# A decoder layer in fp32: softmax scalings made for two query blocks at once, and the next group's left weights moved behind an operand in a load queue

## The chip, the cores and the metric

The kernel runs on one core of a Trainium2 chip. The metric is the time of one execution on the device in microseconds (us); less is better. A core has TensorE (PE, matrix products; PEld is its loading of weights), VectorE (DVE), ScalarE (ACT), GpSimd (POOL) and SyncE (SP), which here only issues loads and stores. Each engine works through its own instructions in order and waits for others by semaphores.

## What is computed

The reference is one inference step of a decoder layer with 1024 prompt tokens and 8 sample tokens of width 1024, all in fp32. Three parts add to the residual: a mixer whose input projection feeds four heads of differential attention and four of retention, a cross-attention into 256 memory tokens, and a squared-ReLU MLP with 4096 hidden rows. The change touches the first and the last:

```python
def diff_attention(q, k, v, q_pos, k_pos, rel_bias, lam):
    q1, q2 = q[..., :DK_A], q[..., DK_A:]
    k1, k2 = k[..., :DK_A], k[..., DK_A:]
    ...
    def probs(qi, ki):
        s = jnp.einsum('bqhd,bkhd->bhqk', qi, ki).astype(f32) * scale + bias
        return jax.nn.softmax(jnp.where(mask, s, neg), axis=-1)

    attn = probs(q1, k1) - lam * probs(q2, k2)
    return jnp.einsum('bhqk,bkhd->bqhd', attn, v.astype(f32))

def sq_relu_mlp(h, w_up, w_down):
    return jnp.square(jax.nn.relu(h @ w_up)) @ w_down
```

The heads' outputs are then divided by their root mean square (`head_rms`).

## The kernel before

Every fp32 product is made of three matmuls on halves: an operand is split into a rounded high half (a cast on ACT) and the rest (a subtraction on DVE), here UH/UL, wh/wl, KA/KB or ah/al.

**The softmax stage** lies at about 250 to 416 us. The prompt attention works per head `h`, query block `q` of 128 rows and map `m` (0 and 1) in `scores` (L1006): PE makes the scores `sp` in PSUM, with one instruction DVE adds the bias and mask `M` and finds the row's extreme (L1019), and ACT takes the exponential with the row sums `sm` (L1025). After map 1, DVE makes a factor per row, lambda times one sum over the other, by a reciprocal (L1032) and a small scalar_tensor_tensor (L1033), and adds the scaled second map to the first (L1034), so that one unnormalized map `e0` is left. `turn` (L1037) transposes `e0` of a pair of blocks on PE (`trA`), splits it into `ah` and `al`, and `weigh` multiplies by the values. When a head is through, ACT squares its output (`sq`, L1077 in `norm_sums`), PE sums the squares by columns (`ct`, in `norm_factors`), and the factors of the norm are spread out again through a transpose (`hrT`).

A loop over 40 steps walks through heads and pairs and interleaves these pieces with other work (projections of the following heads, `qkp`, retention). The order of PE's matmuls is pinned to the program's; the other engines are ordered by a scheduler, under the waits that data and buffers make. Tiles come from rings: `mn` (maxima and factors) has four, the second maps `e1` have two, which the squares `sq`, and the later `rbh` and `diag` share.

**The down projection** is the last stage, from 1133 us on. Its products are made over quadrants in the manner of Strassen: seven products q = 1 to 7, on sums of quadrants of the weights (left) and of the hidden rows (right, in the scratch HQ and HT in DRAM). A loop runs over four groups `g` of 1024 hidden rows. `load_left` loads a group's eight left tiles `raw_d` (512 KB each, L2492); `right_lower` loads a right operand in two halves `raw_h` (516 KB each, L2375), from a ring of three tiles, casts (L2381) and subtracts (L2382); `left_lower` splits a left tile (L2388, L2389); `lower` makes twelve matmuls (L2412) into a bank `dn`, and DVE adds the bank to a quadrant `c` of the output (L2546). The quadrants begin with the residual, which SP loads (`c<-X3`, L2361). All these loads stand in SP's one queue. Where the program says `issue_after(x)`, the scheduler puts an instruction behind x; `seen["SP"]` is the last load that `right_lower` or `load_left` issued. In group 0 the operands come in the order 1, 2, 6, 7, 4, 5, 3.

## Time and profile before

| | |
|---|---|
| median of 3 runs | 1473.42 us (1473.18 to 1474.27) |
| the profiled execution | 1475.19 us |
| its span | 1473.4 us |
| mean granted clock of TensorE | 0.996 |
| instructions | 28129 |
| moved by DMA | 238.98 MB, mean 162 GB/s |

The span reaches from the first to the last instruction of the profiled execution; what lies around it makes up the rest of its time. A row of the timeline gives start, duration, engine, line of the kernel, operation, output<-inputs with their sizes, and in brackets the idle time ahead of it with what ended that. PE and PEld rows overlap, as matmuls are pipelined. The granted clock is the share of TensorE's full rate. SPq rows are the issue of loads, not their running.

### The profile page before, as it was taken

The numbers are of one execution on the slowest core, as the hardware profiler recorded it, in microseconds if no ns is written. First come the engines' busy times: TensorE is split into PE (matmuls) and PEld (weight loads), VectorE is DVE, ScalarE is ACT, GpSimd is POOL, SyncE is SP. The second block draws the span as 40 slices with busy tenths as digits, with TensorE's granted clock in tenths as the row PEclk, the third lists the DMA queues.
The fourth block names the chain that finished last, engine by engine and source line by source line (L and its number), as shares of the span: only waits on it lengthen the run. The fifth ranks groups of instructions, "written<-read, shape, count | busy, mean of one in ns | idle before, by whom it ended". The sixth has DMA issues, their size and how long they took to land.

```text
span 1473.4 us, 28129 instructions
## 1 busy us (share of the span) xinstructions
PE 1455.7 (99%) x11013; PEld 1401.0 (95%) x11013; DVE 1107.9 (75%) x2263; ACT 679.7 (46%) x1327; POOL 314.4 (21%) x345
## 2 busy tenths in 40 slices
PE   9999999999999999999999999999999999999998
PEld 7899779999889999999999999999999999999998
DVE  7666536888867756567868988888888878787876
ACT  7434435666552441267436533343435443343454
POOL 0035433122304511224122000000002211110380
PEclk9999999999999999999999999999999999999998
DMA  8155738215957265654762444333446764536273
GB/s 295 62 188 171 205 70 192 72 34 159 283 169 269 100 209 170 177 178 122 236 234 77 151 159 158 138 136 133 149 159 216 262 213 144 173 105 200 71 130 116
DMA packets 129833, 238.98 MB, mean 162 GB/s; under 512 B 13606, under 2 KB 80987, under 8 KB 129572
## 3 DMA queue, kind: packets, MB, share of 16 engines
q1 hardware_dynamic: 91354, 170.66, 36.0%
q0 software_dynamic: 27472, 46.93, 11.8%
q10 hardware_dynamic: 10874, 19.60, 3.5%
q8 instruction: 86, 1.41, 0.4%
q14 instruction: 47, 0.39, 0.1%
HBM read 171.13 MB, written 58.92 MB: 156 GB/s over the span
## 4 chain that ended last, share of the span: by engine, by line
PE 88%; DVE 5%; DMA 2%; ACT 2%; issue 1%; POOL 0%; ACTq 0%; SPq 0%; DVEq 0%
PE dn L2412 20%; PE Z L2244 9%; PE qkp L75 6%; PE Y L2244 6%; PE X L2244 6%; PE mq L75 6%; PE pr_m L75 6%; PE pr_o L75 5%; PE grp L75 3%; PE sp L75 2%; PE mv L75 2%; PE mk L75 1%; PE av L75 1%; PE mpv L75 1%; PE vap_z L524 1%; PE vrp_z L524 1%
## 5 line engine op out<-in xcount | busy, mean ns | idle before, releaser
L2412 PE MATMUL dn<-UH,wd 128*128 128x258 f32 (+1 forms) x1800 | 326.6, 283 | 3.0 <-DVE c L2546 3.0
L2412 PEld LDWEIGHTS dn<-UH,wd 128*128 128x128 f32 x1800 | 279.6, 190 | 3.6 <-ACT wd L2388 2.6
L2412 PE MATMUL dn<-UL,wd 128*128 128x258 f32 x900 | 254.6, 283 | 0.0
L2412 PEld LDWEIGHTS dn<-UL,wd 128*128 128x128 f32 x900 | 170.5, 189 | 0.1
L2546 DVE TENSOR_TENSOR c<-c,dn 128x258 f32<-128x258 f32 (+1 forms) x217 | 89.1, 417 | 38.5 <-PE dn L2412 35.8
L2270 ACT ACTIVATE hq<-r 128x258 f32<-128x258 f32 x128 | 53.7, 421 | 117.4 <-DVE r L2269 117.3
L2244 PE MATMUL Z<-T_h,wu 128*128 128x258 f32 x512 | 98.1, 283 | 0.0
L2244 PE MATMUL X<-UH,wu 128*128 128x258 f32 x512 | 97.5, 282 | 0.0
L2388 ACT CAST wd<-raw_d 128x512 fp32r<-128x512 f32 x96 | 58.7, 619 | 82.0 <-PE dn L2412 77.3
L2052 ACT CAST wu<-raw_up 128x512 fp32r<-128x512 f32 x96 | 59.0, 616 | 61.0 <-PE Z L2244 52.6
L2381 ACT CAST UH<-raw_h 128x1032 fp32r<-128x1032 f32 x56 | 58.7, 1055 | 55.2 <-PE dn L2412 27.9
L2244 PEld LDWEIGHTS X<-UH,wu 128*128 128x128 f32 x512 | 81.3, 188 | 0.0
L2244 PEld LDWEIGHTS Z<-T_h,wu 128*128 128x128 f32 x512 | 81.3, 189 | 0.0
L2382 DVE TENSOR_TENSOR UL<-raw_h,UH 128x1032 fp32r<-128x1032 f32 x56 | 72.9, 1301 | 9.9 <-ACT UH L2381 9.9
L2389 DVE TENSOR_TENSOR wd<-raw_d,wd 128x512 fp32r<-128x512 f32 x96 | 72.3, 759 | 10.2 <-ACT wd L2388 10.2
L2281 POOL DMA_DIRECT2D HT<-ht x32 | 17.2, 536 | 292.1 <-DVE ht L2280 291.6
L2244 PE MATMUL Z<-T_l,wu 128*128 128x258 f32 x256 | 72.3, 282 | 0.0
L2244 PE MATMUL X<-UL,wu 128*128 128x258 f32 x256 | 72.3, 282 | 0.0
L129 ACT CAST wh_u<-raw_u 128x1024 fp32r<-128x1024 f32 x43 | 44.7, 1047 | 57.6 <-PE mq L75 39.9
L2053 DVE TENSOR_TENSOR wu<-raw_up,wu 128x512 fp32r<-128x512 f32 x96 | 64.8, 689 | 3.6 <-ACT wu L2052 3.6
L2402 POOL TENSOR_TENSOR raw_d<-raw_d,raw_d 128x512 f32<-128x512 f32 x16 | 22.1, 1384 | 197.0 <-DVE raw_d L2398 145.3
L130 DVE TENSOR_TENSOR wl_u<-raw_u,wh_u 128x1024 fp32r<-128x1024 f32 x39 | 48.6, 1257 | 20.2 <-ACT wh_u L129 20.0
(616 smaller groups left out, 4707.4 us busy)
## 6 DMA issues: line engine op xcount, KB each, us to landing
raw_u<-in_wall SPq DMA_DIRECT2D x49, 512.0 KB
HT<-ht POOLq DMA_DIRECT2D x32, 516.0 KB, 3.0
raw_h<-HT SPq DMA_DIRECT2D x32, 516.0 KB
raw_up<-in_wall SPq DMA_DIRECT2D x32, 512.0 KB
raw_d<-in_wall SPq DMA_DIRECT2D x32, 512.0 KB
HQ<-hq ACTq DMA_DIRECT2D x32, 387.0 KB
raw_h<-HQ SPq DMA_DIRECT2D x24, 516.0 KB
cmk<-in_cmk SPq DMA_DIRECT2D x16, 512.0 KB
```

Of the source, the lines that this page charges most:

```text
L75: pinned(nc.tensor.matmul(out, l, r, start=start, stop=stop))
L130: (lo_engine or nc.vector).tensor_sub(wl[:, :n], raw[:, :n], wh[:, :n].bitcast(F32))
L2052: nc.scalar.copy(w[:, :512], src)
L2053: nc.vector.tensor_sub(w[:, 512:], src, w[:, :512].bitcast(F32))
L2244: pinned(nc.tensor.matmul(ps, l, r[:, k, :], start=first and k == 0 and x == 0, stop=k == 3 and x == 2, skip_group_check=True))
L2270: nc.scalar.activation(h[:, PLACE[quad], :], r, AF.Square)
L2381: nc.scalar.copy(h, rv)
L2382: nc.vector.tensor_sub(l, rv, h.bitcast(F32))
L2388: nc.scalar.copy(w[:, :512], src)
L2389: nc.vector.tensor_sub(w[:, 512:], src, w[:, :512].bitcast(F32))
L2412: pinned(nc.tensor.matmul(ps[:, part], l, r[:, k, cq], start=first and k == 0 and x == 0, stop=k == 3 and x == 2, skip_group_check=True))
L2546: nc.vector.tensor_add(y, y, ps)
```

## The change

The reciprocal and the small product of L1032 and L1033 are made once for a pair of blocks, on two columns, after map 1 of the odd block; the two scalings of the pair (in the changed kernel L1037) follow there. In the down projection the left tiles of group 1 are placed behind group 0's last operand load.

```diff
             if m:
-
-                e0 = es[h, q][0]
-                nc.vector.reciprocal(mn[:, 2:3], sm[:, 1, q : q + 1])
-                nc.vector.scalar_tensor_tensor(mn[:, 3:4], mn[:, 2:3], nlam, sm[:, 0, q : q + 1], ALU.mult, ALU.mult)
-                nc.vector.scalar_tensor_tensor(e0[:, :n], e[:, :n], mn[:, 3:4], e0[:, :n], ALU.mult, ALU.add)
+                es[h, q] += (e,)
+            if m and q % 2:
+                nc.vector.reciprocal(mn[:, 2:4], sm[:, 1, q - 1 : q + 1])
+                nc.vector.scalar_tensor_tensor(mn[:, 2:4], mn[:, 2:4], nlam, sm[:, 0, q - 1 : q + 1], ALU.mult, ALU.mult)
+                for x in range(2):
+                    e0, _, e1 = es[h, q - 1 + x]
+                    w = P * (q + x)
+                    nc.vector.scalar_tensor_tensor(
+                        e0[:, :w], e1[:, :w], mn[:, 2 + x : 3 + x], e0[:, :w], ALU.mult, ALU.add)
                 seen["E"] = nc.cur_bb.bb.instructions[-1]
...
-            load_left((0, 1) if g == 0 else range(4))
+            with tc.issue_after(seen["SP"]) if g == 1 else nullcontext():
+                load_left((0, 1) if g == 0 else range(4))
```

The order of PE's instructions is the same in both. SP's queue around group 0's last operand (raw_h0_3_0 and raw_h0_3_2), with the next group's left tiles raw_d1, before:

```order
L2375 DMA raw_h0_5_0_14176<-HT_75 128x4x258
L2375 DMA raw_h0_5_2_14180<-HT_75 128x4x258
L2492 DMA raw_d1_0_0_14436<-in_wall 128x1024
L2492 DMA raw_d1_1_0_14438<-in_wall 128x1024
L2375 DMA raw_h0_3_0_14184<-HQ_74 128x4x258
L2492 DMA raw_d1_2_0_14440<-in_wall 128x1024
L2375 DMA raw_h0_3_2_14188<-HQ_74 128x4x258
L2361 DMA c12_13489<-X3_73 128x516 x4
L2492 DMA raw_d1_0_1_14437<-in_wall 128x1024
L2492 DMA raw_d1_3_0_14442<-in_wall 128x1024
L2375 DMA raw_h1_1_0_14452<-HQ_74 128x4x258
```

And in the changed kernel:

```order
L2379 DMA raw_h0_5_2_14148<-HT_75 128x4x258
L2379 DMA raw_h0_3_0_14152<-HQ_74 128x4x258
L2379 DMA raw_h0_3_2_14156<-HQ_74 128x4x258
L2365 DMA c12_13457<-X3_73 128x516 x4
L2496 DMA raw_d1_0_0_14404<-in_wall 128x1024
L2496 DMA raw_d1_0_1_14405<-in_wall 128x1024
L2496 DMA raw_d1_1_0_14406<-in_wall 128x1024
L2496 DMA raw_d1_1_1_14407<-in_wall 128x1024
L2496 DMA raw_d1_2_0_14408<-in_wall 128x1024
L2496 DMA raw_d1_3_0_14410<-in_wall 128x1024
L2379 DMA raw_h1_1_0_14420<-HQ_74 128x4x258
L2496 DMA raw_d1_2_1_14409<-in_wall 128x1024
```

Three left tiles stood in these rows ahead of raw_h0_3_2, and a fourth, raw_d1_1_1, farther up; now all eight stand behind it. Six stand ahead of the next group's first operand raw_h1_1_0, as before, but in one run, and a seventh has moved ahead of that operand's second half.

ACT at the end of head 0, where its square sq_0 is made while head 1's last blocks are under way (e_1_7_1 is map 1 of head 1's block 7), before:

```order
L1025 ACTIVATE e_1_7_0_3422,sm_1_2936<-e_1_7_0_3422,mn_1_7_3423 128x1024
L1077 ACTIVATE sq_0_3464<-oraw_0_2753 128x1024
L1052 CAST ah_1_2_1_3487<-trA_1_2_1_3482 128x512
L967 CAST KA1_2_3473<-kraw_2_3127 64x688
L1025 ACTIVATE e_1_7_1_3448,sm_1_2936<-e_1_7_1_3448,mn_1_7_3423 128x1024
L1052 CAST ah_1_2_2_3536<-trA_1_2_2_3532 128x384
```

And in the changed kernel:

```order
L1025 ACTIVATE e_1_7_0_3405,sm_1_2928<-e_1_7_0_3405,mn_1_7_3406 128x1024
L967 CAST KA1_2_3457<-kraw_2_3116 64x688
L1056 CAST ah_1_2_1_3471<-trA_1_2_1_3466 128x512
L1025 ACTIVATE e_1_7_1_3431,sm_1_2928<-e_1_7_1_3431,mn_1_7_3406 128x1024
L1081 ACTIVATE sq_0_3448<-oraw_0_2746 128x1024
L1056 CAST ah_1_2_2_3520<-trA_1_2_2_3516 128x384
```

The square has moved behind the exponential of block 7's second map.

DVE at the same place, where head 1's block 6 is scaled (e_1_6_0<-e_1_6_1), before:

```order
L1033 SCALAR_TENSOR_TENSOR mn_1_6_3370<-mn_1_6_3370,nlam_88,sm_1_2936 128x1
L1019 ISA e_1_7_0_3422,mn_1_7_3423<-sp_1_7_0_1_3428,M_1_2934,mn_1_7_3423 128x512
L1019 ISA mn_1_7_3423 128x1
L1034 SCALAR_TENSOR_TENSOR e_1_6_0_3369<-e_1_6_1_3394,mn_1_6_3370,e_1_6_0_3369 128x896
L1019 ISA e_1_7_1_3448,mn_1_7_3423<-sp_1_7_1_0_3449,M_1_2934 128x512
```

And in the changed kernel, where the small instructions are on two columns:

```order
L1032 RECIPROCAL mn_1_7_3406<-sm_1_2928 128x2
L1091 TENSOR_TENSOR c8_1_4067<-c8_1_4067 128x8
L1033 SCALAR_TENSOR_TENSOR mn_1_7_3406<-mn_1_7_3406,nlam_88,sm_1_2928 128x2
L1037 SCALAR_TENSOR_TENSOR e_1_6_0_3355<-e_1_6_1_3380,mn_1_7_3406,e_1_6_0_3355 128x896
L1037 SCALAR_TENSOR_TENSOR e_1_7_0_3405<-e_1_7_1_3431,mn_1_7_3406,e_1_7_0_3405 128x1024
```

The scaling of block 6 has moved behind all four reductions of block 7.

## The prediction

> **What bounds the kernel now.** I read the busy table of the page first.

> ```profile
> PE 1455.7 (99%) x11013; PEld 1401.0 (95%) x11013; DVE 1107.9 (75%) x2263; ACT 679.7 (46%) x1327; POOL 314.4 (21%) x345
> ```

> TensorE (PE) is busy for 1455.7 of 1473.4 us. The change takes no matmul away and leaves their order as it was, so work that it saves on another engine counts only where PE stands waiting for it. The second view is therefore the list of PE's waits (line waited for, total us, times, longest).

> ```profile
> PE dn L2412 <- DVE c L2546: 3.0, 2, 2.4
> PE trA L78 <- DVE e L1034: 2.1, 2, 1.4
> PE sp L75 <- DVE mn L1019: 1.8, 2, 1.0
> PE pr_half L75 <- DVE x_half L1356: 0.6, 1, 0.6
> ```

> The first belongs to the down projection, the others to the softmax stage and the step behind it. Third, the timeline of PE gives each of these gaps its place; the bracket is the idle time ahead of the row and who ended it.

> ```profile
> 262.42 0.41 PE L75 MATMUL sp<-KA,Q 128*128 128x320 f32 x1 [0.85 <-DVE mn L1019]
> 350.06 0.55 PE L78 MATMUL trA<-ident,e 128*128 128x128 f32 x3 [0.73 <-DVE e L1034]
> 390.33 0.41 PE L75 MATMUL sp<-KA,Q 128*128 128x320 f32 x1 [0.98 <-DVE mn L1019]
> 395.97 0.55 PE L78 MATMUL trA<-ident,e 128*128 128x128 f32 x3 [1.40 <-DVE e L1034]
> 414.71 0.42 PE L75 MATMUL pr_half<-UH,wh_u 128*128 128x344 f32 x1 [0.61 <-DVE x_half L1356]
> 1188.26 0.36 PE L2412 MATMUL dn<-UH,wd 128*128 128x258 f32 x1 [2.38 <-DVE c L2546]
> ```

> All that the change can win on PE is in these few places. The largest gap costs more than its own length, as PE's rows behind it and two rows of the windows view show (us, busy time of PE, PEld, DVE, ACT, POOL, granted clock, DMA share, GB/s).

> ```profile
> 1189.17 0.41 PE L2412 MATMUL dn<-UL,wd 128*128 128x258 f32 x1
> 1192.39 0.37 PE L2412 MATMUL dn<-UL,wd 128*128 128x258 f32 x1
> 1192.59 0.40 PE L2412 MATMUL dn<-UH,wd 128*128 128x258 f32 x2
> 1192.95 0.40 PE L2412 MATMUL dn<-UH,wd 128*128 128x258 f32 x2
> 1189.20:1192.40 3.20, 3.20 (x18) 3.20 (x17) 2.06 (x5) 0.00 (x0) 0.00 (x0) 0.50 1.04 376
> 396.60:399.60 3.00, 3.00 (x33) 2.54 (x32) 3.00 (x12) 1.51 (x3) 0.01 (x1) 1.00 1.06 407
> ```

> In the fifth row the granted clock is 0.50. From 1189.17 to 1192.39 the pattern of one UL and two UH matmuls runs five times, so 15 matmuls take 3.22 us, 0.215 each; from 1192.59 to 1192.95 three take 0.36, 0.120 each. The 15 would have taken 1.80 at that pace: 1.42 lost, and 0.08 more with the one that still starts 0.20 ahead of its successor. So the gap of 2.38 brought 1.5 more, 3.9 in all. The last row shows the clock at 1.00 right behind the gap of 1.40 at 395.97: not every gap brings it.

> [...]

> **Part two of the change, the queue of the down projection.** What ends the gap at 1188.26 is the addition into `c`, L2546, and I followed it back through the timelines of ACT, DVE and SP's queue, then the landings in the chain of waits.

> ```profile
> 1185.46 1.05 ACT L2381 CAST UH<-raw_h 128x1032 fp32r<-128x1032 f32 x1 [1.11 <-DMA raw_h<-HQ]
> 1186.55 1.23 DVE L2382 TENSOR_TENSOR UL<-raw_h,UH 128x1032 fp32r<-128x1032 f32 x1 [0.18 <-ACT UH L2381]
> 1187.70 0.42 DVE L2546 TENSOR_TENSOR c<-c,dn 128x258 f32<-128x258 f32 x1
> 1174.51 0.38 SPq L2375 DMA_DIRECT2D raw_h<-HQ  x1
> 1174.93 0.51 SPq L2492 DMA_DIRECT2D raw_d<-in_wall  x1
> 1177.60 0.38 SPq L2375 DMA_DIRECT2D raw_h<-HQ  x1
> 1170.01 5.21 DMA raw_h<-HT
> 1177.60 7.84 DMA raw_h<-HQ
> 1180.10:1185.90 5.80, 5.78 (x49) 5.58 (x47) 2.04 (x3) 2.02 (x3) 0.00 (x0) 1.00 0.78 279
> ```

> The last operand's second half, raw_h0_3_2, is issued at 1177.60 and lands 7.84 later. Its cast and the subtraction UL follow, and in DVE's order the addition of dn_7_2_0 stands behind that subtraction, though it needs nothing of it. PE wants the bank's result at 1185.88 (1188.26 less 2.38) and gets it only then. By SP's order three left weights of the next group, 0.5 MB each, stand close ahead of this load. The change puts all eight behind raw_h0_3_2: the first half still goes at 1174.51, and the second can follow as soon as its slot is free, some 0.5 us earlier at 1177.1 since the queue does nothing in between. The load before them, with little beside it, took 5.21. With that duration, and not 7.84, it lands at 1182.3; at the 279 GB/s of the windows row, the 1.5 MB that no longer run ahead are 5.4 us less, which gives 1180.0. The chain behind it has measured 1188.12 less 1185.44, 2.7 us: the addition ends at 1182.7 to 1185.0, and PE asks at 1185.9. The wait goes, with 0.9 to 3 us to spare. I take the whole **-3.9**; the bounds are -3.9 and, if the second half keeps its landing, 0.

> What is late next? The eight weights now start behind four pieces of c12, and the next group's operands raw_h1_1_0 and raw_h1_1_2 stand behind six and seven of them on SP. In PE's order the first matmul that needs raw_h1_1_2 comes some 11 steps of 12 matmuls (1.45 us each at 0.120) behind 1185.9, at about 1201.9, and cast and subtraction want it landed by 1199.1. From 1174.5 on 6.8 MB must come through (four operand halves of 0.53, c12 with 1.06, seven weights of 0.52): 280 GB/s. I charge nothing, and say below what it costs if that rate fails.

> **Part one, the scaling once per pair.** These are the two removed kinds by the group view of the softmax stage, and one that stays.

> ```profile
> L1033 DVE SCALAR_TENSOR_TENSOR mn<-mn,nlam,sm 128x1 f32<-128x1 f32 x32 | 6.9, 216 | 0.2
> L1032 DVE RECIPROCAL mn<-sm 128x1 f32<-128x1 f32 x32 | 5.1, 160 | 2.1 <-ACT e L1025 2.0
> L1034 DVE SCALAR_TENSOR_TENSOR e<-e,mn,e 128x896 f32<-128x896 f32 x4 | 4.6, 1146 | 0.1
> ```

> Half of the 64 small ones go: 16 x (0.160 + 0.216) = 6.0 us of DVE, with those on 128x2 priced like those on 128x1. PE waits for DVE in this stage for only a few us, so most of the 6.0 lies beside other work. Gap by gap, by DVE's order in the changed program: the one at 262.42 loses the scaling that stood ahead of its reduction (-0.6 of 0.85); those at 350.06 and 395.97 lose a pair of small ones (-0.2 each); the one at 390.33 gets a scaling placed ahead of it (+0.3); at 414.71 the work left over is less (-0.6). That is **-1.3**. Bounds: all five gaps gone, -4.6, and +1 if the later scaling delays a transpose.

> The cost is in a wait that the trace of before does not have. The square `sq` of a head shares the two slots of `e1` with the second maps. In both programs its slot comes free with the scaling of block 6 of the next head. That scaling now waits for block 7's exponential and for the pair's factor. PE's column sums `ct`, in a fixed place, need `sq`. Heads 1 and 2:

> ```profile
> 320.17 0.60 PE L78 MATMUL trA<-ident,e 128*128 128x128 f32 x4
> 320.10 1.05 ACT L1077 ACTIVATE sq<-oraw 128x1024 f32<-128x1024 f32 x1
> 321.05 0.57 ACT L1052 CAST ah<-trA 128x512 fp32r<-128x512 f32 x1
> 322.43 1.15 ACT L1025 ACTIVATE e<-e,mn 128x1024 f32<-128x1024 f32 x1
> 323.49 0.19 ACT L1025 ACTIVATION_READ_ACCUMULATOR e<-e,mn 128x1 f32 x1
> 322.74 1.84 PE L75 MATMUL ct<-ones,sq 128*128 128x1 f32 x16
> 364.26 1.06 ACT L1077 ACTIVATE sq<-oraw 128x1024 f32<-128x1024 f32 x1
> 366.36 1.15 ACT L1025 ACTIVATE e<-e,mn 128x1024 f32<-128x1024 f32 x1
> 366.77 1.84 PE L75 MATMUL ct<-ones,sq 128*128 128x1 f32 x16
> ```

> Before, `sq` began ahead of the exponential of block 7 and `ct` found it ready. After, for the first pair of rows: the transposes end at 320.77, the cast 0.57 gives 321.4 (ACT's order now has it ahead of the exponential), exponential 1.15 + 0.19, reciprocal 0.16, factor 0.22, scaling 1.15, square 1.05: 325.3 against 322.74, so PE waits 2.5. For the next head the exponential can start about 1.6 earlier than its 366.36, since DVE has three instructions fewer ahead of it (0.16 + 0.22 + 1.15): 364.8, plus 1.15 + 0.19 + 0.16 + 0.22 + 1.15 + 1.06 = 3.93, is 368.7 against 366.77: 2.0. Together **+4.5**. If neither exponential starts earlier than it did, they come to 322.43 + 3.92 - 322.74 = 3.6 and 366.36 + 3.93 - 366.77 = 3.5, that is 7.1; if the instructions overlap by 0.1 each, as the two starts 322.43 and 323.49 of a 1.15 do, 3.3. I take 4.5, the value that follows the new order. Work behind `ct` on PE is in order and cannot step in.

> A gap of 2.38 brought the half clock, one of 1.40 did not. Of the new gaps one is longer and one lies between. I count it once: **+1.5**; bounds 0 and 3.0. [...]

> **The sum.** -3.9 - 1.3 + 4.5 + 1.5 = +0.8. On the profiled execution, 1475.19 with a span of 1473.4, that makes 1476.0 and a span of 1474.2. It lies 1.77 above the median of the runs, 1473.42; the same +0.8 there gives **1474.2**.

> **Rivals.**
> 1. *No half clock behind the new gaps.* The 1.40 gap with its clock of 1.00 speaks for it, the 2.38 gap against: -3.9 - 1.3 + 4.5 = -0.7, 1472.7. [...]
> 2. *Half clock behind both.* -3.9 - 1.3 + 4.5 + 3.0 = +2.3, 1475.7; with the longer waits of the upper bound, +4.9, 1478.3.
> 3. *Slower: the wait comes back one group later.* If the transfers hold less than 280 GB/s, raw_h1_1_2 lands late; at 260 the 6.8 MB end at 1200.7, and as its issue also waits for slots, some 2.1 behind 1199.1. Then PE stands 2.1 and runs at half clock for 1.5, and 3.6 of the 3.9 is given back: +4.4, 1477.8. The 279 above speaks for it, the 376 against. The same sum results if the first wait stays.
> 4. *Faster: DVE's relief reaches every gap.* The softmax gaps go whole and neither `ct` draws the half clock: -3.9 - 4.6 + 4.5 = -4.0, 1469.4. That both `sp` gaps are ended by the reduction behind the scaling speaks for it; that the scalings now come two at a time speaks against.
> 5. *The change does nothing on DVE's side* because the pairing is hidden whole and `ct` finds another slot: -3.9, 1469.5. The slot's release is fixed by the ring of two, which speaks against.

> **How the numbers follow.** What a measurement of this kernel can tell from no change is about 0.2%, 2.9 us. Chances: forecast 0.32, rival 1 0.18, rival 2 0.17 (0.10 of it within 0.2%), rival 3 0.18 (slower), rival 4 0.10 and rival 5 0.05 (both faster). No case within 0.2% is left out but that of the longer `ct` waits, 0.03 of the forecast's 0.32, which is slower. So faster 0.15, same 0.32 - 0.03 + 0.18 + 0.10 = 0.57, slower 0.07 + 0.18 + 0.03 = 0.28. The range holds the forecast and rivals 1, 2 and 3; it leaves out rivals 4 and 5 (0.15) and the upper end of rival 2 (about 0.04): 1470.0 to 1478.0.

> **What would show it.** Right: no gap above 0.5 us at the step of 1188; two gaps ahead of `ct`, 2 to 3 us each, ended by ACT's `sq`; a granted clock of 0.50 behind at least one. Wrong: `ct` without a wait, or with more than 3.6; gaps at the start of group 1 ended by `UL`; gaps of the softmax stage that stay as they are, or go whole.

## The result and the profile after

| | median, us | runs |
|---|---|---|
| before | 1473.30 | 1472.53 to 1474.27, 4 runs |
| changed | 1491.65 | 1490.89 to 1496.19, 4 runs |

The ratio is 1.0131, 95% interval 1.011 to 1.0152: 18.4 us slower, where 0.8 us was forecast and 1478.0 was the upper end of the range. The profiled execution of the changed kernel took 1496.19 us with a span of 1494.4, the longest of the four. Medians and ratios below leave out one execution of 2869.56 us in run 9, which the record doesn't explain.

The page of the changed kernel, busy time of each engine:

```profile
PE 1465.8 (98%) x11013; PEld 1408.9 (94%) x11013; DVE 1104.7 (74%) x2231; ACT 680.2 (46%) x1327; POOL 310.5 (21%) x345
```

PE executes the same 11013 matmuls in the same order and is busy 10.1 us longer than its 1455.7 before. So matmuls ran slower. The other half of the loss stands in the list of PE's waits:

```profile
PE trA L78 <- DVE e L1037: 5.9, 5, 3.4
PE ct L75 <- ACT sq L1081: 5.0, 2, 2.8
PE av L75 <- DVE al L1057: 2.1, 1, 2.1
PE dn L2416 <- DVE c L2551: 1.9, 4, 0.6
PE sp L75 <- DVE mn L1019: 1.3, 2, 0.7
```

Before, `trA` waited 2.1, `ct` not at all, `av` 0.3 and `sp` 1.8. So the softmax stage and the step behind it wait 10.1 us more (3.8 + 5.0 + 1.8 - 0.5). In the down projection the wait of 2.4 is gone, and four of up to 0.6 stand there, of which the last, 0.6 at the end of the stage, was there before. The timeline of PE gives the places:

```profile
326.41 2.15 PE L75 MATMUL ct<-ones,sq 128*128 128x1 f32 x16 [2.82 <-ACT sq L1081]
354.90 0.30 PE L78 MATMUL trA<-ident,e 128*128 128x128 f32 x1 [0.79 <-DVE e L1037]
356.51 0.55 PE L78 MATMUL trA<-ident,e 128*128 128x128 f32 x3 [1.30 <-DVE e L1037]
376.00 3.58 PE L75 MATMUL ct<-ones,sq 128*128 128x1 f32 x16 [2.22 <-ACT sq L1081]
409.76 0.31 PE L78 MATMUL trA<-ident,e 128*128 128x128 f32 x1 [3.38 <-DVE e L1037]
430.42 0.43 PE L75 MATMUL pr_half<-UH,wh_u 128*128 128x344 f32 x1 [0.61 <-DVE x_half L1360]
446.03 0.38 PE L75 MATMUL av<-al,VH 128*128 128x256 f32 x1 [2.13 <-DVE al L1057]
786.15 0.75 PE L75 MATMUL pr_m<-UH,wh_u 128*128 128x258 f32 x4 [0.26 <-ACT UH L2175]
1209.56 0.36 PE L2416 MATMUL dn<-UH,wd 128*128 128x258 f32 x1 [0.34 <-DVE c L2551]
```

The `pr_half` row stood at 414.71 before: 15.7 us are lost by then. The row at 1209.56 is the matmul that stood at 1188.26, 21.3 later. The two waits at `ct` are those that were predicted, 2.8 and 2.2 for 2.5 and 2.0. The second `ct` also takes 3.58 us instead of 1.84. The windows view (us, busy time of PE, PEld, DVE, ACT, POOL, granted clock, DMA share, GB/s), put where PE's rows lie twice as far apart:

```profile
328.00:331.40 3.40, 3.40 (x15) 3.34 (x15) 0.94 (x5) 0.50 (x2) 1.66 (x1) 0.50 0.03 5
375.80:379.20 3.40, 3.20 (x15) 3.20 (x16) 1.36 (x2) 1.08 (x2) 0.62 (x2) 0.50 0.52 108
379.20:382.60 3.40, 3.40 (x13) 3.40 (x14) 2.34 (x4) 0.00 (x0) 1.61 (x2) 0.50 0.17 36
409.92:413.32 3.40, 3.13 (x12) 2.99 (x12) 2.87 (x8) 1.63 (x5) 0.00 (x0) 0.50 1.04 396
447.47:450.87 3.40, 3.40 (x17) 3.27 (x16) 0.56 (x1) 0.48 (x1) 0.00 (x0) 0.50 0.11 36
788.80:792.20 3.40, 3.40 (x18) 3.40 (x17) 1.24 (x1) 0.53 (x1) 0.00 (x0) 0.50 0.00 0
```

Six windows of half clock, 3.4 us each, against one before, besides the 0.50 at the end of both spans (from 1488.5 here and from 1465.6 before). Each costs up to half its length by its clock of 0.50, 1.7, so five more make by this estimate some 8.5 of the 10.1; the rest I did not assign. The waits of the softmax stage and the step behind it and the longer busy time together give 20.2 of the 21.0 by which the two spans differ. The rest is mainly what the memory stage waits more (`mtr` from 0.2 to 1.1 and two new waits of 0.3 and 0.4) less the 0.6 that the down projection waits less.

### The profile page after: what moved, and what is told of

The parts are those of the page before. It is cut to its first block, busy times and chain, and to the rows that moved or that the text cites. A ratio compares the mean times of both kernels' runs of the same rounds, so it can differ in the third digit from the quotient of the medians.

```text
span 1494.4 us, 28120 instructions
## 1 busy us (share of the span) xinstructions
PE 1465.8 (98%) x11013; PEld 1408.9 (94%) x11013; DVE 1104.7 (74%) x2231; ACT 680.2 (46%) x1327; POOL 310.5 (21%) x345
## 4 chain that ended last, share of the span: by engine, by line
PE 81%; DVE 8%; DMA 5%; ACT 3%; issue 2%; ACTq 0%; POOL 0%; SPq 0%; DVEq 0%
PE dn L2416 17%; PE Z L2248 9%; PE qkp L75 6%; PE pr_m L75 6%; PE X L2248 6%; PE Y L2248 6%; PE mq L75 5%; PE pr_o L75 5%; PE grp L75 3%; PE sp L75 1%; PE av L75 1%; PE mpv L75 1%; PE vap_z L524 1%; PE vrp_z L524 1%; DMA raw_h<-HQ 1%
## 5 line engine op out<-in xcount | busy, mean ns | idle before, releaser
L75 PE MATMUL qkp<-UH,wh_u 128*128 128x344 f32 x192 | 63.9, 333 | 0.1
```

What stands on the lines that cost most here:

```text
L75: pinned(nc.tensor.matmul(out, l, r, start=start, stop=stop))
```

## The experiments

All medians stand beside runs of the kernel before on the same chip, which gave 1473.2 to 1473.3 in each set. Theory A puts the loss into the new waits of the softmax stage with the half clock behind them; B and the others stand in the texts.

**1. The queue alone.** The kernel before, with part two of the change alone.

> The kernel before with part two alone (the left weights of group 1 behind raw_h0_3_2). Theory A, the loss is part one's and part two gains: the gap of 2.38 us and its half clock of 1.5 go, the four small gaps that the changed kernel shows in the down projection (0.53, 0.34, 0.59, 0.32 us) come, so 1473.3 - 3.9 + 1.8 = 1471.2 us, 1470 to 1472. Theory B, part two carries part of the loss, since the eight weights collide with the next group's operands: 1473.3 us or more.

Measured: 1473.58 us against 1473.29, ratio 1.0004 (0.9995 to 1.0013). The time lies in theory B's range, but the interval holds no change at all: the loss that B means isn't there, nor are the 2 us of gain that A counted on. Its profiled execution has no wait at the old place, 0.6 at the end of the stage and 1.0 near its start (`dn` waiting for ACT's `c`).

**2. The pairs alone.** The changed kernel with the load queue of before (part two taken back).

> The changed kernel with the queue of before (part one alone). Theory A: the whole loss and part two's gain on top, 1491.7 + 2.1 = 1493.8 us, 1492 to 1496, with the gap of 2.4 us in the down projection back. Theory B: clearly under 1490 us.

Measured: 1491.83 us against 1473.29, ratio 1.0136 (1.0119 to 1.0153). Part one is the whole loss; the time is just under the 1492 at which theory A's range begins. The gap of 2.4 in the down projection, which should have come back with the old queue, did not: `dn` waits 0.6 in all, at the end of the stage.

**5. The kernel before, profiled again**, since the first two runs left the gap in doubt.

> The kernel before, unchanged, profiled once more. Theory F, the gap of 2.38 us at 1188 was an event of that one execution and not of the kernel, which is why part two alone gave 1473.58 against 1473.29: no gap over 0.6 us at the same place (between the first matmuls of q = 4 in group 0), profiled time 1471 to 1474 us. Theory G, the gap belongs to the kernel and part two trades it for something else: a gap of 2 us or more there again.

Measured: 1471.85 us, in one execution. Theory F for this execution. Its waits, its second issue of `raw_h` and the casts behind, from three views:

```profile
PE dn L2412 <- DVE c L2546: 0.6, 1, 0.6
```

```profile
1178.72 0.38 SPq L2375 DMA_DIRECT2D raw_h<-HQ  x1
```

```profile
1183.51 1.06 ACT L2381 CAST UH<-raw_h 128x1032 fp32r<-128x1032 f32 x1 [1.11 <-DMA raw_h<-HQ]
```

The 0.6 stands at the end of the stage. The same load, with the same three left weights ahead of it, took 4.8 us from issue to cast instead of 7.86, and PE ran through. A gap of 2.38 belonged to one execution. But theory F goes too far when it calls the gap no matter of the kernel, as PE's rows at the same matmul in runs 9 and 10 show, which have the old queue too:

```profile
1196.87 0.36 PE L2415 MATMUL dn<-UH,wd 128*128 128x258 f32 x1 [1.15 <-DVE c L2549]
1190.82 0.36 PE L2415 MATMUL dn<-UH,wd 128*128 128x258 f32 x1 [0.43 <-DVE c L2549]
```

At this matmul the six executions with the old queue wait 2.38, 0, 0, 1.15, 0.43 and 0, which is 0.7 on average, and of the seven with the new queue one waits 0.34 and the others at most 0.1. So the new queue does nearly clear this place, but `dn` waits elsewhere instead: near the start of the stage, for ACT's `c`, six of the seven wait 0.5 to 1.0, against one of the six with 0.4. Over all profiled executions `dn` waits 3.0, 0.6, 0.6, 1.8, 1.2 and 2.2 us with the old queue (before, its repetition, and runs 2, 9, 10 and 11) and 2.4, 1.6, 2.2, 1.7, 2.9, 1.5 and 1.8 with the new one (changed, runs 1, 3, 4, 6, 7, 8). In sum the new queue takes nothing off.

**3. The last pair single.** The changed kernel, where blocks 6 and 7 are scaled one by one, so that the slot of `e1` comes free as it did before:

```diff
-            if m and q % 2:
+            n_ = 2 if q < 6 else 1
+            if m and (q % 2 or n_ == 1):
```

(with the columns and the loop running over `n_` blocks).

> The changed kernel, but blocks 6 and 7 of each head are scaled one by one as before; pairs 0 to 5 stay paired. Theory A, the two waits at ct come from the slot of the ring of two that the last pair holds longer: both waits (2.8 and 2.2 us) go, and three windows of half clock behind them (about 1.6 us each): 1491.7 - 9.8 = 1482 us, 1480 to 1484; the waits of trA at 355 and 410 stay. Theory C, sq is late for another reason (ACT's order), and only the place of the wait changes: 1489 us or more.

Measured: 1479.75 us against 1473.29, ratio 1.0042 (1.0025 to 1.0059): 11.9 less than the changed kernel, and a little under theory A's range. Both waits at `ct` are gone, and the wait of 2.1 at `av` with them, which I had not counted; one stretch of half clock is left in the stage (mean granted clock 0.997, in the changed kernel 0.991).

**8. Only the last pair**, the reverse (`n_ = 2 if q > 5 else 1`).

> Only blocks 6 and 7 of each head are paired, the rest is scaled one by one as before. Theory A: the two waits at ct with their half clock, and the wait of av (2.1 us) that went with them, come back alone: 1473.3 + 12 = 1485 us, 1482 to 1487; no wait over 1.5 us at trA. Rival: the small pairs carry most of the loss: under 1479 us.

Measured: 1483.34 us against 1473.18, ratio 1.0077 (1.006 to 1.0094). Its list of waits:

```profile
PE ct L75 <- ACT sq L1084: 5.0, 2, 2.8
PE trA L78 <- DVE e L1040: 2.1, 2, 1.4
```

Theory A: `ct` waits its 5.0, and `trA` is back at the 2.1 of before. The wait at `av`, which theory A let come back too, did not. Four stretches of half clock stand behind `ct` and farther on (mean granted clock 0.993). So the last pair costs 10 to 12 us, and the pairs below it 6.5.

**4. Filling the wait.** The changed kernel with

```diff
             ct = PS.tile([P, 512], F32, tag="tr", name=f"ct_{h}", bufs=2)
+            if h < 2:
+                for _ in range(10):
+                    mm(ct, vals[h + 1][0][:, :P], vals[h + 1][0][:, :512], True, True)
```

> [...] Theory D, the half clock follows from how few columns stream through TensorE in a window of 3.4 us: the wait for sq stays in time, but one to three of the three windows of half clock go: 1487 to 1490 us. Theory E, the half clock follows from the wait itself, or PE isn't idle there for that long: 1491.7 us or more, with 0.50 behind both ct as before.

Measured: 1485.49 us against 1473.29, ratio 1.0083 (1.0068 to 1.0099): 6.2 less than the changed kernel, though twenty matmuls were added, 4.6 us by estimate from the 0.229 that one takes in run 10. `sq` still waits for its slot, but PE has work until it comes, all but 0.5 us at the first `ct`; in the profiled execution two windows of half clock are left in the whole stage where five were (mean granted clock 0.996 for 0.991). Theory D, by a little more than its range. Not all of the 6.2 need be the clock's: the longest wait at `trA` is 2.2 here instead of 3.4.

**6. The decode instruction later.** In the changed kernel DVE's row ahead of the wait of 3.38 at `trA` is not the scaling:

```profile
404.56 0.17 DVE L1032 RECIPROCAL mn<-sm 128x2 f32<-128x2 f32 x1
408.28 0.21 DVE L1232 TENSOR_SCALAR dmn<-dmn,qblkd 128x1 f32<-128x1 f32 x1 [3.55 <-DMA qblkd<-in_sel]
408.41 0.21 DVE L1033 SCALAR_TENSOR_TENSOR mn<-mn,nlam,sm 128x2 f32<-128x2 f32 x1
409.00 1.28 DVE L1037 SCALAR_TENSOR_TENSOR e<-e,mn,e 128x384 f32<-128x384 f32 x2
```

Between the reciprocal and the factor of blocks 2 and 3 stands an instruction of the decode step that waits for a load. DVE stood 3.55 us in front of it. The scheduler had it behind the reciprocal of block 4 before, where the load had landed. The edit:

```diff
-            nc.vector.tensor_scalar(mn[:, 2:3], mn[:, 2:3], second, 1.0, ALU.mult, ALU.add)
+            with tc.issue_after(seen["E"]):
+                nc.vector.tensor_scalar(mn[:, 2:3], mn[:, 2:3], second, 1.0, ALU.mult, ALU.add)
```

> The changed kernel, with the small decode instruction that waits for the load in_sel put behind the pair's scaling in DVE's order. Theory A: the wait of 3.4 us at trA falls to 1 us or less and the half clock behind it goes, 1491.7 - 2.4 - 1.6 = 1487.7 us, 1485.5 to 1489.5. Rival: the wait at trA is the pair's own chain (odd block's exponential, factor, two scalings) and only its name changes: 1491 us or more.

Measured: 1487.86 us against 1473.18, ratio 1.0105 (1.009 to 1.012). Theory A. `trA` now waits:

```profile
PE trA L78 <- DVE e L1037: 3.5, 4, 1.3
```

The wait at this place is 1.28, a little over the 1 us that theory A allowed. Of 5.9, 2.4 were this one load's; 3.5 remain, against 2.1 before. The wait at `av` is 1.0 here instead of 2.1, so not all of the gain is `trA`'s.

What remains need not be the pair's order alone. The wait that the kernel before has not is that of 1.30 at 356.51 in the changed kernel (1.31 here), and ahead of it DVE's two scalings take long. The changed kernel's scalings of blocks 2 and 3, what GpSimd does meanwhile, and the scaling of the same block 2 before:

```profile
353.08 3.38 DVE L1037 SCALAR_TENSOR_TENSOR e<-e,mn,e 128x384 f32<-128x384 f32 x2
353.06 1.28 POOL L995 TENSOR_TENSOR VL<-vraw,VH 128x512 fp32r<-128x512 f32 x1 [5.04 <-ACT VH L993]
354.65 1.26 POOL L995 TENSOR_TENSOR VL<-vraw,VH 128x512 fp32r<-128x512 f32 x1 [0.31 <-ACT VH L993]
347.02 0.62 DVE L1034 SCALAR_TENSOR_TENSOR e<-e,mn,e 128x384 f32<-128x384 f32 x1
```

The two took 1.68 and 1.77 us, where the shortest of their widths took 0.61 and 0.74. In the traces of the kernel before and the changed one 4 of the 64 scalings, two in each, took over 0.1 us longer than the shortest of their width: 1.32 and 1.81 before, 1.68 and 1.77 here. All 4 ran beside this subtraction (`VL`, L995) of GpSimd for 1.2 us or more, and none of the others did for more than 0.6. Without the 2.1 us that the two lost, the wait of 1.30 would not be there; that is worked out, as no run moved the subtraction.

**7. Both mends**, the last pair single and the decode instruction later.

> Both mends: blocks 6 and 7 scaled one by one, pairs below stay paired, and the decode instruction behind the scaling. Theory A: from 1479.75 another 2.2 us of wait less about 0.8 that the pair's chain keeps, and one window of half clock of 1.6: 1476.7 us, 1475 to 1478, still above the kernel before by the waits of trA behind pairs 0 to 5. Rival: with both waits gone the saved DVE work shows: 1472 us or less.

Measured: 1476.62 us against 1473.18, ratio 1.0023 (1.0013 to 1.0034). Theory A: the saved DVE work doesn't show even with both waits at `ct` and the long one at `trA` gone. `trA` waits 3.5 in all and `pr_half` 1.4 instead of 0.6.

**11. Only the first pair**, queue of before (`n_ = 2 if q < 2 else 1`).

> Queue of before, only blocks 0 and 1 of each head paired. Theory A: no slot held longer at the heads' ends and the shortest scalings (0.35 and 0.48 us) delayed; eight small instructions, 1.5 us of DVE, go where PE mostly doesn't wait: 1472.5 to 1473.5 us. Rival: the placement of other instructions by the scheduler shifts with any such edit and costs on its own: 1474.5 us or more.

Measured: 1473.90 us against 1473.28, ratio 1.0006 (0.9997 to 1.0015). No difference that can be told, between the two theories' ranges. No version that was run beats the kernel before.

**9 and 10. Few columns or many, without a wait.** The kernel before, for head 0, ahead of `ct`, with either of

```diff
+                for x in range(16):
+                    mm(ct[:, x + 8 : x + 9], sq[:, x % 8 * P : x % 8 * P + P], ones[:, :1], True, True)
```

```diff
+                for _ in range(17):
+                    mm(ct, vals[h + 1][0][:, :P], vals[h + 1][0][:, :512], True, True)
```

> The kernel before, with sixteen more products of one column ahead of ct of head 0 (results unread): by ct's 1.84 us for eight, 3.7 us more in which TensorE never waits but streams almost no columns. Theory D, the half clock follows from the columns that stream in a window of 3.4 us: 0.50 follows without any wait, 1473.2 + 3.7 + 1.6 to 3.2 = 1478.5 to 1480 us. Theory E, it follows from waiting: 1476.9 us with the clock at 1.00.

> [...] Both theories: 1473.2 + 3.6 = 1476.8 us, clock 1.00 behind; under theory D this is 1.6 to 3.2 us less than the run with narrow products, under theory E the same as it.

Measured: 1481.31 us with the narrow products, the median of three executions (ratio 1.0054, 1.0035 to 1.0072), and 1476.02 with the wide ones (1.0021, 1.0011 to 1.0031), against 1473.28. The narrow kernel's timeline at this place, and its windows:

```profile
322.98 6.94 PE L75 MATMUL ct<-ones,sq 128*128 128x1 f32 x48
```

```profile
323.20:326.60 3.40, 3.40 (x33) 3.40 (x32) 0.67 (x2) 0.71 (x2) 1.19 (x4) 1.00 1.04 248
326.60:330.00 3.40, 3.40 (x18) 3.40 (x18) 0.05 (x1) 0.00 (x0) 0.00 (x0) 0.50 0.37 59
330.00:333.40 3.40, 3.40 (x14) 3.34 (x15) 2.75 (x9) 1.14 (x3) 2.69 (x1) 0.50 0.00 0
```

The wide kernel's:

```profile
322.42 4.06 PE L75 MATMUL ct<-VH 128*128 128x512 f32 x17
326.32 1.84 PE L75 MATMUL ct<-ones,sq 128*128 128x1 f32 x16
```

```profile
326.50:329.90 3.40, 3.40 (x28) 3.38 (x29) 0.34 (x2) 0.48 (x1) 1.25 (x1) 1.00 0.15 21
```

PE is busy without a gap in both. Behind the products of one column the clock is 0.50 for two windows, behind the matmuls of 512 columns it stays 1.00. The 3.6 us in the sum of run 10 are shown by no run: the seventeen stand from 322.42 to 326.32, 3.90 us, 0.229 each. The two kernels differ by 5.3 us, though the narrow products add 3.7 by `ct`'s 1.84 for eight and the wide ones 3.9, so theory D. It expected 3.2 at most: part of the narrow products run at half clock themselves (6.94 us for 24 columns, 5.5 by `ct`'s 1.84). Farther on, each of the two profiles has one more window of half clock, at 398.3 and at 770.3, where PE's rows lie nearly twice as far apart (344 columns 0.29 instead of 0.16, 258 columns 0.21 instead of 0.12).

## Why the prediction was wrong

**Term by term**, forecast against what the traces show: the queue -3.9 and 0 (run 1); the softmax gaps -1.3 and +3.3 (`trA` 3.8 more, `sp` 0.5 less); the waits at `ct` +4.5 and +5.0; the half clock +1.5 and some +8. The wait at `av`, 1.8 more, was in no term. That adds up to about 18, against 18.4 between the medians.

**The two waits at `ct` were right**: place, releaser and size (2.8 and 2.2 for 2.5 and 2.0). Experiment 3 takes them away, and experiment 8 brings them back. They follow from the ring of two and the later scaling of block 6, for which ACT stands idle ahead of the first square:

```profile
325.30 1.06 ACT L1081 ACTIVATE sq<-oraw 128x1024 f32<-128x1024 f32 x1 [1.74 <-DVE e L1037]
```

**The half clock was the term that was mis-sized.** I counted it once behind two waits, +1.5, on the argument that a gap of 1.40 had not brought it and one of 2.38 had. Behind `ct` it came for three windows, and in the stage and the step behind it for five, some 8 us; the sixth, at 788.8, lies elsewhere. The step that failed took the gap's length for the cause. In run 9 two such windows came without a gap, behind 3.4 us in which PE ran 33 matmuls of one column each, and in run 10 the clock stayed at 1.00 with 17 matmuls of 512 columns at the same place. `ct` itself is sixteen instructions of one column, so the wait of 2.8 and `ct` together left 15 columns in the 3.4 us ahead of the stretch at 328.0, and the second `ct` itself ran in a window of half clock, behind which a second one follows.

**The -1.3 for the softmax gaps had the wrong sign.** It was read from DVE's order at the five gaps of before, by counting small instructions. At `trA` two scalings now follow the odd block's exponential where one did, and run 6, with no load in the way, shows 3.5 us of wait where 2.1 stood. These 1.4, less the 0.5 that `sp` did gain, are within the prediction's bound of +1; the 2.4 of the load go beyond it. The new wait is that behind blocks 2 and 3, where both scalings ran beside GpSimd's subtraction and took more than twice their time (1.68 and 1.77 for 0.61 and 0.74), which an order of instructions doesn't show.

**One row of DVE's order was left out**: the decode instruction with its load, behind the reciprocal of blocks 2 and 3 where it stood behind that of block 4. It made the largest wait (3.38), and a window of half clock follows; moving it away gave 3.8 us back, with 1.1 of wait at `av` among it.

**The -3.9 for the queue failed**, and by the trace that it rested on. The wait was real in that execution, and its chain was read rightly, but its size was that one execution's. The old queue costs 0.7 at this place on average of six executions, with one window of half clock in the six; the new one clears it and makes other waits of that size, and the queue alone changes nothing (1.0004). The profiled execution lay 1.77 above the median, which the prediction noted and did not use; the repetition, without the gap and its half clock, took 1471.85. A transfer that took 7.84 once and 4.8 the next time had been taken for a property of the queue.

**The saving of DVE time**, put at 6.0 us and mostly hidden, was right in kind: the two small lines went from 6.9 and 5.1 us to 3.5 and 2.6, and no run shows a gain from it. DVE's busy time as a whole can't tell: 1104.7 in the changed kernel, 1107.9 and 1106.0 in the two executions of the kernel before, and 1104.4 in run 1, which leaves this stage as it was.

**Rivals.** Rival 2, half clock behind both waits, is what happened, and more: even with the longer waits it stood at 1478.3. Rival 3 did not come: no wait of the changed kernel's down projection is over 0.6. Rivals 1, 4 and 5 are refuted.

**Open.** Why `av` waits 2.1 at 446.03 in the changed kernel, and neither with the last pair single (run 3) nor with the last pair alone (run 8): DVE's rows ahead of it are in another order in run 3, and no run moved these alone. Nor was it tried to keep the pairs and give `sq` a place of its own, or to move GpSimd's subtraction. Why `mtr` waits 1.1 in the changed kernel and in run 8, and 0.2 before, was not followed.

## What to carry to other kernels

Merging small work of two blocks makes the first block wait for the second; ask which buffers the first one holds meanwhile, who stands in line for their slots, and what the merged work will run beside. The size of a wait in one profiled execution is a property of the kernel only when a second one shows it too, above all when it hangs on a transfer and the execution lies above the median. Where a scheduler orders an engine, look in the new order for instructions that wait on loads and have moved ahead of work that PE needs.

## What the runs showed of the hardware

I counted the columns of the matmuls that begin in each step of this grid, in the kernel before, the changed one and runs 9 and 10, behind the first 10 us and ahead of the end at 0.50. A middling step has 7,224 in the changed kernel and in the kernel before. In the kernel before 0.50 followed a step of 1,806 (at 1185.7), and the poorest that 1.00 followed has 3,272 (at 421.1). In the changed kernel 0.50 followed steps of 15 (at 324.6, and at 375.8, itself at 0.50), 128 (406.5), 2,656 (372.4), 2,958 (785.4) and 3,000 (444.1), and the poorest that 1.00 followed has 3,104 (at 437.2). In run 9 0.50 followed some 30 (at 323.2) and some 360 (at 326.6, itself at 0.50), but also 3,650 (at 394.9), and 1.00 followed 3,440 (at 429.0); the step of 3,650 holds a cluster of sixteen `dsc` products of 128x16 by 128. So the columns tell most of it in these traces but not all. The group view of the step ahead of the stretch at 788.8 shows a cluster of narrow products, by the row that fills more than half of it:

```profile
L75 PE MATMUL opm<-selgt,daccm 128*128 128x8 f32 x16 | 1.9, 245 | 0.0
```

The only gap in that step is the 0.26 at 786.15. The kernel before has the same sixteen products and the same gap of 0.26, at 764.91, and ran on at full clock:

```profile
766.90:770.30 3.40, 3.40 (x29) 3.40 (x30) 1.44 (x2) 1.15 (x2) 0.00 (x0) 1.00 0.00 0
```

The two differ in where the grid falls. In the changed kernel the sixteen lie in one step, but for 3 ns of the first, and in run 10 all of them do (2,708 columns, at 766.9); 0.50 followed in both. In the kernel before the grid cuts them into 9 and 7, in run 9 into 4 and 12, and 1.00 followed. Counted from the start of the span, the first step begins at 1.31 us in the kernel before and at 0.32 in the changed one, so the grid's place was another in each of these two executions.
